# Ten gate tiles as five pairs of seven half-size products, and attention with one more pair in flight

## The chip, the core and the metric

The kernel runs on one core of a Trainium2 chip. The core has a matrix engine (TensorE, PE in the profile, its weight loads PEld), a vector engine (VectorE, DVE), an activation engine (ScalarE, ACT), a general engine (GpSimd, POOL) and a queue engine (SyncE, SP) that issues nearly all DMAs here. Engines run their own instruction streams in order and meet at semaphores. Matmuls write to the eight banks of PSUM; everything else lies in SBUF, in slabs of 128 partitions by 1032 float32.

The metric is the device time of one execution in microseconds, as a median of runs.

## The reference

One step of one layer of a decoder trunk, for a prompt of 1024 tokens and 8 sample tokens, in float32:

```
h = RMSNorm(x)
qa,ka,va,za, qb,kb,vb,zb, qc,zc, ga,gb,gc = split(h @ w_in)
y = x + W_out( sum_i sigmoid(g_i) * P_i( mixer_i(h) * silu(z_i) ) ),   i = A, B, C
```

Mixer A is dilated causal attention with 8 heads of 64 and three patterns of window and stride, mixer B sliding-window attention with 8 query heads on 2 key heads and a sink per head, mixer C attention into 256 memory tokens with 4 heads of 128. The sample tokens attend to caches of keys and values. The step also returns the new keys and values. What matters here: the gates g are three matrices of 1024 x 1024 columns of w_in, applied to all 1032 tokens (1024 of the prompt and 8 of the sample), and each only ever enters through its sigmoid, which the kernel makes from a tanh.

## The kernel before

Activations are kept transposed, features on partitions and tokens along the row. A matrix product in the kernel is a "tile": 128 output features for all 1032 tokens, in three chunks of CH = 344 tokens, with the contraction of 1024 in 8 blocks of 128. To hold float32 precision with the fast float32 format, each operand is split into a rounded high half and a remainder (`hh`, `hl` for activations, `wh`, `wl` for weights), and three of the four partial products are summed (`PARTS`, `order`, `fm`). A tile is therefore 3 chunks x 8 blocks x 3 = 72 matmuls of 344 columns, each with its own weight load. A branch tile has half the contraction.

The program is written out by a planner in Python. `Pace` is a model of the engines' clocks; `tick` is called between half chunks of a tile and issues side work when the model says that its inputs are there: a step of attention (`rope`), a step of the sample's attention (`samp`), weight fetches and splits (`wahead`, `wnext`, `wpump`), and callbacks left with `when`, which are tried at each tick. What is issued runs in that order on each engine; the model decides the order alone, while semaphores keep the data right.

The order of the dense work on TensorE is: memory keys and values; queries of C; then a list of jobs for B and A, with `fill` (12 z tiles, then 24 gate tiles) in between where a job isn't allowed yet; the remaining fill; then three branches (C, B, A: `branch`, 8 tiles each with 36 matmuls of 344 columns) and the output matrix (`out_phase`). `plan` inside `main` appends the weights of the next job when fewer than two weights are left in the list `W`, and appends the tail's weights (branches and output) once jobs and fill are used up. Weights are fetched `wdepth` ahead and split `wsoon` ahead.

A gate tile (`gate`) takes any of six PSUM banks in turn once attention is over (`dense`, `wide`), writes tanh of each chunk into a slab `sg`, and stores the slab to DRAM (`gsc`). The branches load it back later.

Attention runs in pairs of query blocks (`DuoC`, `DuoN`, `DuoR`; 112 in all). Each goes through a pipeline in `rope`: scores on TensorE into the one bank `psSc` (`s`), bias and softmax on DVE and ACT into `L` (`soft`), transposes into `psT` (`t_prev`, `t`), rounding and remainder of the probabilities (`hi`, `lo`), the product with values into `psO` (`pv`), and the eviction (`fin`). In `self.pipe = (new, p1)` two pairs are in flight: at each step the pair before the new one is transposed, and the one before that is multiplied with values. A step is skipped when the model says that `p1.L` or `p2.pl` isn't there yet. Up to three heads' inputs lie in slabs.

The sample's attention (`sample`, `samples`) is done on POOL (products `ck<-ck,qbc`, `cv<-cv,pb`) and DVE (reductions). After prompt attention has ended, two such samples run side by side, their row buffers in a slab (`late`), with all three key blocks fetched at once (`deep`).

The first branch needs mixer C's output times silu(z), split in halves (`y_fetch(2)`: loads `yr` and `zr` for four tiles, two at a time, product, split into `yh` and `yl`). It is called in `main` when fewer than four entries of fill are left.

`SLABS = 47` slabs are shared by all of this, and a slab is free again when the last Python name for it is dropped.

## Time and profile before

| | |
|---|---|
| median of 3 runs | 1166.72 us (1164.03 to 1168.59) |
| the profiled execution's own time | 1162.82 us |
| its span, first to last instruction | 1161.0 us |
| mean granted TensorE clock | 0.990 |
| DMA over the span | 206.29 MB, 178 GB/s |
| gate tiles: first and last store | 572.60 and 926.24 us |
| branches: stores of the gates loaded back | 926.7 to 1022.6 us |

Every helper of the kernel is recorded under one line (L150), so the profile is read by the names of tiles: `psD<-hh,wh` is a matmul that writes bank psD from activations hh and weights wh. Busy times of PE overlap from one matmul to the next, so the length of one matmul in a row (some 320 ns for 344 columns) is longer than the distance from one start to the next. `<-` behind a bracket names what ended an engine's idle time. SPq is the time that SP takes to issue a DMA, not the transfer.

### The profile page before, as it was taken

How to read it: one execution, taken by the hardware profiler on the slowest of the kernel's cores; microseconds unless marked ns; L12 is line 12 of the kernel's file. 1: busy time of each engine (PE TensorE's matmuls, PEld its weight loads, DVE VectorE, ACT ScalarE, POOL GpSimd, SP SyncE). 2: the span in 40 equal slices, each digit the busy share in tenths (PEclk: the TensorE clock that was granted, in tenths of full speed). 3: DMA queues.
4: the chain of work that ended last, by engine and by line, in shares of the span. 5: the costliest groups of instructions: out<-in, count | busy, mean ns of one | idle time of the engine just before them, and what ended most of it. 6: DMA issues, size and time to landing. Idle time of an engine off the chain costs nothing.

```text
span 1161.0 us, 19631 instructions
## 1 busy us (share of the span) xinstructions
PE 1125.8 (97%) x7424; PEld 1104.7 (95%) x7424; DVE 645.7 (56%) x1201; ACT 475.1 (41%) x1136; POOL 503.2 (43%) x402
## 2 busy tenths in 40 slices
PE   7899999999899999999999999999999999999998
PEld 7787999999899999999999999999999999999998
DVE  6754366444566867655755765643647447538211
ACT  6443355544555556556555455541212212213000
POOL 4454455232543232345235314423557665857200
PEclk8998999999999999999999999999999999999999
DMA  8312522399624555544654664648699699532332
GB/s 319 119 43 79 182 75 92 102 306 302 201 74 147 182 164 168 193 155 141 185 133 134 191 177 163 192 136 293 214 265 382 186 350 374 165 137 73 119 119 73
DMA packets 85794, 206.29 MB, mean 178 GB/s; under 512 B 13588, under 2 KB 38130, under 8 KB 85700
## 3 DMA queue, kind: packets, MB, share of 16 engines
q1 hardware_dynamic: 85556, 205.03, 54.6%
q8 instruction: 58, 0.95, 0.3%
q14 instruction: 36, 0.29, 0.1%
q10 hardware_dynamic: 144, 0.02, 0.0%
HBM read 154.98 MB, written 45.97 MB: 173 GB/s over the span
## 4 chain that ended last, share of the span: by engine, by line
PE 78%; DVE 6%; DMA 5%; POOL 4%; issue 3%; ACT 2%; SPq 1%; POOLq 0%; ACTq 0%; DVEq 0%
PE psD L150 46%; PE psO L150 14%; PE psSc L150 9%; PE psM L150 5%; PE psT L150 5%; DMA wr<-w_in 1%; DVE ml L150 1%; SPq L150 1%; DVE wl L150 1%; POOL sq L150 1%; DMA vhl<-vhl 1%; POOL c L150 1%; DMA bn<-rep 1%; DMA wr<-w_mk 1%; POOL wl L150 1%
## 5 line engine op out<-in xcount | busy, mean ns | idle before, releaser
L150 PE MATMUL psD<-hh,wh 128*128 128x344 f32 x1184 | 386.0, 326 | 3.9 <-DVE sz L150 1.7
L150 PE MATMUL psD<-hh,wl 128*128 128x344 f32 x1184 | 380.7, 322 | 4.7 <-DVE wl L150 4.7
L150 PE MATMUL psD<-hl,wh 128*128 128x344 f32 x1184 | 381.1, 322 | 2.3 <-POOL hl L150 1.4
L150 PEld LDWEIGHTS psD<-hh,wh 128*128 128x128 f32 x1184 | 224.1, 189 | 6.8 <-DVE sz L150 1.9
L150 PEld LDWEIGHTS psD<-hh,wl 128*128 128x128 f32 x1184 | 224.2, 189 | 5.3 <-DVE wl L150 5.3
L150 PEld LDWEIGHTS psD<-hl,wh 128*128 128x128 f32 x1184 | 224.4, 190 | 4.0 <-POOL hl L150 2.7
L150 POOL TENSOR_TENSOR wl<-wr,wh 128x1024 fp32r<-128x1024 f32 (+1 forms) x45 | 106.3, 2362 | 50.6 <-ACT wh L150 48.4
L150 ACT ACTIVATE p<-psT 128x512 fp32r<-128x512 f32 (+2 forms) x112 | 61.8, 552 | 93.5 <-PE psT L150 81.1
L150 DVE TENSOR_TENSOR wl<-wr,wh 128x1024 fp32r<-128x1024 f32 (+1 forms) x54 | 72.9, 1354 | 42.7 <-ACT wh L150 21.5
L150 ACT ACTIVATE wh<-wr 128x1024 fp32r<-128x1024 f32 (+1 forms) x62 | 54.7, 888 | 89.1 <-DMA wr<-w_out 36.9
L150 POOL TENSOR_TENSOR c<-raw 128x344 f32<-128x344 f32 x51 | 43.4, 851 | 96.1 <-ACT raw L150 85.8
L150 POOL TENSOR_TENSOR ck<-ck,qbc 128x1024 f32<-128x1024 f32 x24 | 65.3, 2733 | 39.6 <-DMA qbc<-d 21.6
L150 POOL TENSOR_TENSOR cv<-cv,pb 128x1024 f32<-128x1024 f32 x24 | 58.4, 2440 | 53.6 <-DMA pb<-d 28.8
L150 DVE TENSOR_TENSOR p<-psT,p 128x512 fp32r<-128x512 f32 (+2 forms) x112 | 70.7, 631 | 14.1 <-ACT p L150 13.4
L150 POOL TENSOR_SCALAR wh<-wr 128x1024 fp32r<-128x1024 f32 (+1 forms) x37 | 41.1, 1111 | 73.1 <-DMA wr<-w_in 43.6
L150 PE MATMUL psT<-ident,L 128*128 128x128 f32 x400 | 72.4, 272 | 0.0
L150 ACT ACTIVATE L<-L,sta 128x256 f32<-128x256 f32 (+1 forms) x128 | 59.5, 467 | 27.6 <-DVE sta L150 27.4
L150 POOL TENSOR_TENSOR sg<-sg,sg 128x344 f32<-128x344 f32 x48 | 55.1, 1155 | 34.4 <-DVE sg L150 19.4
L150 DVE CUSTOM_DVE_ANT_0 L<-psSc,bias 128x256 f32<-128x256 f32 (+1 forms) x128 | 43.7, 378 | 42.9 <-PE psSc L150 42.4
L150 ACT ACTIVATE sq<-psD 128x344 fp32r<-128x344 f32 x51 | 23.3, 457 | 74.7 <-PE psD L150 66.9
L150 POOL TENSOR_TENSOR sq<-c,sq 128x344 fp32r<-128x344 f32 x51 | 52.0, 1020 | 4.0
L150 PEld LDWEIGHTS psT<-ident,L 128*128 128x128 f32 x400 | 48.7, 140 | 0.2
(284 smaller groups left out, 2539.6 us busy)
## 6 DMA issues: line engine op xcount, KB each, us to landing
wr<-w_in SPq DMA_DIRECT2D x58, 512.0 KB
g<-sg SPq DMA_DIRECT2D x24, 516.0 KB
sg<-g SPq DMA_DIRECT2D x24, 516.0 KB
pb<-d SPq DMA_DIRECT2D x32, 256.0 KB
rb<-d SPq DMA_DIRECT2D x26, 258.0 KB
qbc<-d SPq DMA_DIRECT2D x12, 512.0 KB
z<-sz SPq DMA_DIRECT2D x12, 512.0 KB
wt<-d SPq DMA_DIRECT2D x24, 256.0 KB
```

Source lines behind the costliest of these rows:

```text
L150: r = f(*a, **k)
```

## The change

**Pairs of gate tiles.** The last gate tiles are computed two at a time. Two tiles are 256 output features; with the contraction of 1024 in two halves of 512 and the 1032 tokens in two halves of HT = 516, they are eight block products of 128 features x 512 x 516. The change computes them with seven products (Strassen's method in Winograd's form): sums and differences of blocks of the weights and of the activations are multiplied, and sums of the products give the four results. Each product is two token parts of 258 columns x 4 blocks x 3 partial products = 24 matmuls of 258 columns.

- `mix` (new) makes three sums of the activations' blocks (T1, T2, T4: 12 slabs `ht`) after attention has ended, while ordinary gate tiles still run, and sets a flag at its end; `mix_last` writes a fourth (T3) over the second token half of the first four activation slabs when the last ordinary gate is done.
- `pair_fetch` loads the two raw weight tiles, `pair_prep` makes the four sums on POOL and splits one operand after the other into a slab `wx`, `LEAD = 2` products ahead.
- `gate_pairs` runs the seven products, adds them up in PSUM and in slabs `u`, and writes tanh of the results; `gate_out` stores them.
- `plan` takes ordinary gates until the flag is set and their number is even; the rest go in pairs. Ten of the 24 tiles do.
- `y_fetch(2)` is called at the first product of the last pair; its splits wait for a flag `room`, set after that pair's fourth product, where the fetch of the tail's weights begins too.

**Attention.** `self.pipe` holds three pairs, so a pair is transposed two steps after its scores; `L`, `stc`, `stb` and `sta` get a third buffer, and slabs go from 47 to 46.

**Sample.** The side-by-side samples take a slab for their rows only if another one holds the row buffers (`rowbusy`), fetch one key block at a time (`deep = 1`), and a new one is begun only when the one before has been handed out (`feed`).

**z tiles.** tanh is written straight into the slab `sz`.

```diff
-        p1, p2 = self.pipe
+        p0, p1, p2 = self.pipe
...
-        if new and p1 and p1.carry:
-            new.prev = p1
+        if new and p0 and p0.carry:
+            new.prev = p0
...
-        self.pipe = (new, p1)
+        self.pipe = (new, p0, p1)
...
-        late = self.duos is None
-        deep = npat if late else 1
+        late = self.rowbusy
+        deep = 1
...
-            self.when([r], split, t, r)
+            self.when([r], self.after, "room", split, t, r)
...
+    def pair_prep(self, q):
...
+        if q == 0:
+            nc.gpsimd.tensor_add(z[:, :512], b[:, :512], b[:, 512:1024])
+            nc.gpsimd.tensor_sub(z[:, 512:1024], z[:, :512], a[:, :512])
+            src = a[:, :512]
...
+        elif q == 3:
+            y = st["y"] = self.slab(F32, "ws")
+            nc.gpsimd.tensor_sub(y[:, :512], a[:, :512], b[:, :512])
+            nc.gpsimd.tensor_sub(y[:, 512:1024], a[:, 512:1024], z[:, 512:1024])
+            src = a[:, 512:1024]
...
+        x = self.slab(F32R, "wx")
+        self.round(x[:, :512], src)
+        self.rest(x[:, 512:1024], src, x[:, :512])
+        self.pws.append((x[:, :512], x[:, 512:1024]))
+        self.pready += 1
+
+    def gate_pairs(self, pairs):
...
+        steps = (("B11", 0, True), ("T2", 1, True), ("T1", 2, True), ("B21", 0, False), ("T3", 1, False), ("T4", 1, False), ("B22", 2, False))
+        self.mix_last(h)
...
+        for p, pair in enumerate(pairs):
+            bank = [[self.ps("D", 2) for _ in range(2)], [self.ps("O", 2) for _ in range(2)], [self.ps("Sc", 1), self.ps("M", 1)]]
...
+            for q, (key, i, new) in enumerate(steps):
+                while self.pready < min(7 * p + q + LEAD, n):
+                    self.pair_prep(self.pready % 7)
+                if q == 2 and not last:
+                    self.pair_fetch(pairs[p + 1])
+                if q == 0 and last:
+                    self.y_fetch(2)
...
+                for j in range(2):
...
+                    for m, (y, z, k) in enumerate(self.order(4)):
+                        nc.tensor.matmul(b, w[y][:, k * P:(k + 1) * P], x[k][z][:, c], start=new and m == 0, stop=m == 11, skip_group_check=True)
+                    if q == 0:
+                        nc.scalar.activation(u1[:, c], b, AF.Copy)
+                    elif q == 1:
+                        nc.vector.tensor_tensor(u2[:, c], b, u1[:, c], op=ALU.add)
+                    elif q == 4:
+                        nc.vector.tensor_tensor(u3[:, c], b, u1[:, c], op=ALU.add)
+                        nc.vector.tensor_tensor(s2[:, d], bank[2][j][:, :HT // 2], u3[:, c], op=ALU.add)
+                    elif q == 3:
+                        nc.scalar.activation(s1[:, c], b, AF.Tanh, scale=0.5)
+                    elif q == 5:
+                        nc.vector.tensor_tensor(s2[:, c], b, u1[:, c], op=ALU.add)
+                    elif q == 6:
+                        nc.vector.tensor_tensor(s1[:, d], b, u2[:, c], op=ALU.add)
+                    yield
...
+                if q == 3 and last:
+                    self.flags.add("room")
+                    self.begin_tail()
...
-            while (jobs or fill) and len(self.W) - self.wi < 2:
+            while len(self.W) - self.wi < 2:
...
+                elif gates and ("mix" not in self.flags or len(gates) % 2):
+                    x, mt = gates.popleft()
+                    j = ([wi(34 + 8 * x + mt)], None, lambda x=x, mt=mt: self.gate(x, mt))
...
+            if self.duos is None and self.pipe == (None,) * 3 and "mixing" not in self.flags and len(gates) > 5:
+                self.flags.add("mixing")
+                self.mix()
...
+        if gates:
+            gates = list(gates)
+            yield from self.gate_pairs(list(zip(gates[::2], gates[1::2])))
```

## The prediction

> **What bounds the kernel.** I read the page's busy times first, then the busy times by stage, then what TensorE waited for.

> ```profile
> span 1161.0 us, 19631 instructions
> PE 1125.8 (97%) x7424; PEld 1104.7 (95%) x7424; DVE 645.7 (56%) x1201; ACT 475.1 (41%) x1136; POOL 503.2 (43%) x402
> ```

> ```profile
> 0.00:116.00 116.00, 100.17 (x541) 88.19 (x542) 70.08 (x95) 55.31 (x100) 55.43 (x54) 0.91 0.40 140
> 145.00:775.00 630.00, 619.01 (x4304) 613.15 (x4303) 383.13 (x860) 339.82 (x894) 242.65 (x202) 1.00 0.54 165
> 775.00:926.00 151.00, 150.42 (x961) 148.53 (x960) 78.69 (x84) 31.66 (x64) 82.47 (x52) 1.00 0.79 262
> 926.00:1063.00 137.00, 136.33 (x868) 136.07 (x867) 76.78 (x117) 29.77 (x46) 91.46 (x72) 1.00 0.67 237
> 1063.00:1161.00 98.00, 90.92 (x573) 89.78 (x571) 25.91 (x38) 9.87 (x17) 19.20 (x11) 1.00 0.27 92
> ```

> The columns are the length, busy PE, weight load, DVE, ACT and POOL with counts, the granted clock, the DMA share and GB/s. From 145 us on PE is full: attention among dense tiles (145 to 775) idles 11.0 us of 630, the gate tiles after it 0.6 of 151, the branches 0.7 of 137. The clock is at 1.00, so only fewer or shorter matmuls, or fewer waits, can shorten these stages. PE's own waits leave little there:

> ```profile
> PE psD L150 <- DVE wl L150: 5.6, 3, 2.4
> PE psD L150 <- DVE ml L150: 3.7, 3, 1.9
> ...
> PE psSc L150 <- DVE sta L150: 1.7, 2, 1.3
> PE psT L150 <- DVE aw L150: 1.7, 1, 1.7
> ```

> (total, times, longest). A bank that attention's softmax holds (sta) costs 1.7 us in all.

> **The change: the products.** Each gate tile is 72 matmuls of 344 columns. Its store follows its last product, and in a quiet stretch the stores stand one tile apart:

> ```profile
> 809.28 0.33 SPq L150 DMA_DIRECT2D g<-sg  x1
> ...
> 820.60 0.33 SPq L150 DMA_DIRECT2D g<-sg  x1
> ...
> 831.93 0.33 SPq L150 DMA_DIRECT2D g<-sg  x1
> ```

> That is 11.32 us a tile, 157.3 ns a matmul; ten tiles take 113.2 us. In place of them stand 5 pairs x 7 products x 24 = 840 matmuls of 258 columns (two token parts, four blocks of the contraction, three passes of the high and low halves): 168 a pair where there were 144, with a quarter fewer columns each. The trace has 256 columns in attention's scores, each with a weight load of its own:

> ```profile
> 182.61 0.28 PE L150 MATMUL psSc<-mkh,qh 128*128 128x256 f32 x1
> ...
> 183.20 0.28 PE L150 MATMUL psSc<-mkh,ql 128*128 128x256 f32 x1
> ...
> 755.24 0.88 PE L150 MATMUL psO<-p,v 128*128 128x128 f32 x6
> ```
> ```profile
> L150 PE MATMUL psO<-p,v 128*128 128x128 f32 x112 | 20.0, 260 | 0.0
> ```

> Six scores start within 0.59 us, 118 ns apart. The slope to 344 columns is (157.3-118)/88 = 0.45 ns a column, so 258 take 119 ns. Six 128-column products last 0.88 us; with the last one's own length (0.26 us, the mean of that group) taken off, five steps are 124 ns: below 256 columns nothing is won, and 124 is the high end here; the low end is a 256-column row without its two extra columns, 117. So the pairs take 840 x 119 = 100.0 us (98.3 to 104.2): **13.2 us less** (9.0 to 14.9).

> [...]

> **The weights of a pair.** Four sums of 512 columns on POOL and seven roundings and remainders of 512 replace two of 1024. A product's weights are prepared two ahead, and what is issued for product i+1 stands behind the evictions of i-1, so it has about one product, 24 x 119 = 2.86 us.

> ```profile
> L150 ACT ACTIVATE wh<-wr 128x512 fp32r<-128x512 f32 x24 | 14.8, 626 | 47.6 <-DMA wr<-w_brc 26.7 <-POOL sg L150 7.6 <-DVE yl L150 5.7
> L150 DVE TENSOR_TENSOR wl<-wr,wh 128x512 fp32r<-128x512 f32 x14 | 12.3, 880 | 0.0
> L150 POOL TENSOR_TENSOR wl<-wr,wh 128x512 fp32r<-128x512 f32 x12 | 20.7, 1721 | 10.4 <-ACT wh L150 9.7 <-DVE sg L150 0.7
> L150 DVE CUSTOM_DVE_ANT_0 L<-psSc,bias 128x256 f32<-128x256 f32 x88 | 35.2, 420 | 26.0 <-PE psSc L150 26.0
> ```

> Two evictions of 258 columns (2 x 0.42) beside the rounding (0.63), then the remainder on DVE (0.88): 1.7 us; on POOL 0.63 + 1.72 = 2.4. That fits, with 0.5 to 1.1 us to spare. The evictions add ten adds of 0.42 = 4.2 us of DVE a pair, in 20 us, and bank psO is written again one half product (1.43 us) after the product whose sum must first be read from it; two adds, 0.84, fit. What doesn't fit is a remainder that meets one of the sample's POOL products:

> ```profile
> 864.27 3.41 DVE L150 TENSOR_TENSOR wl<-wr,wh 128x1024 fp32r<-128x1024 f32 x1 [4.91 <-POOL wh L150]
> ...
> 870.43 1.21 DVE L150 TENSOR_TENSOR wl<-wr,wh 128x1024 fp32r<-128x1024 f32 x1
> ```

> The first ran while POOL worked on `cv<-cv,pb`, and took 2.2 us more. In this stage the ten such remainders on DVE average

> ```profile
> L150 DVE TENSOR_TENSOR wl<-wr,wh 128x1024 fp32r<-128x1024 f32 x10 | 16.1, 1613 | 28.2 <-POOL wh L150 15.2 <-ACT wh L150 13.1
> ```

> 0.4 us more than the undisturbed 1.21. In before a weight has a whole tile (11 us) of cover; now it has one product. Bounds: 0 (all hidden) to 35 x 0.4 = 14 us. Half of the 35 on DVE would lose 7 us without the spare time; it covers the most of it, so I take **3 us**.

> **From gates to branches.** Before, the first branch's inputs are fetched 58 us ahead of their use; now they are fetched at the start of the last pair, 7 x 2.86 = 20.0 us ahead, and split only after its fourth product.

> ```profile
> 867.81 0.37 SPq L150 DMA_DIRECT2D yr<-y  x1
> ```
> ```profile
> 874.09 1.22 DVE L150 TENSOR_TENSOR yr<-yr,zr 128x1024 f32<-128x1024 f32 x1 [0.63 <-DMA zr<-z]
> ...
> 903.91 1.43 DVE L150 TENSOR_TENSOR yl<-yr,yh 128x1032 fp32r<-128x1032 f32 x1 [1.92 <-ACT yh L150]
> ...
> 949.57 1.23 DVE L150 TENSOR_TENSOR yl<-yr,yh 128x1032 fp32r<-128x1032 f32 x1
> ```
> ```profile
> 876.69 2.39 POOL L150 TENSOR_TENSOR yr<-yr,zr 128x1024 f32<-128x1024 f32 x1 [3.95 <-DMA zr<-z]
> ```
> ```profile
> 879.51 1.06 ACT L150 ACTIVATE yh<-yr 128x1032 fp32r<-128x1032 f32 x1
> ```
> ```profile
> 875.00:900.00 25.00, 25.00 (x162) 24.67 (x161) 18.56 (x12) 7.30 (x12) 21.03 (x9) 1.00 0.97 379
> ```
> ```profile
> 925.56 0.32 PE L150 MATMUL psO<-yh,wh 128*128 128x344 f32 x1
> ```

> The chain took 867.81 to 905.34 = 37.5 us there, with nothing waiting for it. Its bare steps: the second tile lands and POOL begins its product after 8.9 us; that issues the fourth tile's load, another 8.9; product 2.39, rounding 1.06, remainder 1.23 (undisturbed, at 949.57): 23.5 us. PE then waits 23.5 - 20.0 = **3.5 us**; bounds 0 (loads that land faster than under the DMA share of 0.97 in that stretch) and 17.5 (the 37.5 again). The branch weights start at the same point, 3 products = 8.6 us ahead; their load, 0.63 and 0.88 lie inside that, and cost nothing beyond it unless SP's queue holds them up; then they are late beside the inputs, not after them.

> **Mixing the activations, and attention.** Four steps of one add on DVE, one on POOL, differences of 516 columns and three splits run beside two or three ordinary gate tiles, whose weights are two tiles ahead: 0 (bounds 0 and 2). With a third pair in flight, transposes use scores that are two steps old. PE saves at most the 1.7 us of `aw` and 1.7 of `sta` above, and new scores may wait for psSc's reader: 112 pairs at a tenth of 0.42 is 5 us. The pair before last's remainder must still be ready, and DVE issues it behind the reading of psSc, so I take 0 (bounds -3 and +5). Attention ends earlier, and that alone wins nothing: the same tiles are still to be done. It decides how many gates are left for pairs; each pair fewer costs 13.2 / 5 = 2.6 us. The third buffers cost one slab of 47, and the sample fetches one key block ahead instead of three; its last result has a long way to go:

> ```profile
> L150 DVE COPY ys<-sog x12: 171/171/172, 209.4 to 965.3; 128x8 f32<-128x8 f32 x12
> ```

> The last branch, which needs it, begins two branches of 8 x 36 matmuls x 157.3 ns = 45.3 us after 925.56, at 1016.2; 965.5 and a chain of 37.5 us give 1003.0, so some 13 us are to spare, and I take 0.

> **The sum.** -13.2 + 3 + 3.5 + 0 = -6.7 us on the profiled execution's 1162.82 (its span of 1161.0 and 1.8 around it): 1156.1. The median shown, 1166.72, lies 3.9 above that execution; the same difference gives **1160.0 us**.

> **Rivals.** (1) *All is hidden*: preparation and inputs keep up. For it: POOL is busy 82 of 151 us and DVE 79, and loads may land faster. Then -13.2 + 0 to 1: 1154. (2) *The inputs of the first branch are late*, the slower side: the chain of 37.5 us repeats, and PE stands 17.5 us at the head of the branches. For it: it is the one measured length; against: half of it was DVE held up by POOL with nobody waiting. -13.2 + 3 + 17.5 = +7.3: 1174. It decides from a wait of 13.2 - 3 = 10.2 us. (3) *The preparation bounds the products*: remainders held by POOL cost PE 0.4 us each, 14 in all: -13.2 + 14 + 3.5 = +4.3: 1171. Against: the spare time, and either engine may take a remainder. (4) *The spacing follows the number of matmuls*: at 139 ns, midway between 120 and 157, 840 take 116.8 us, +3.6 + 6.5: 1177; it turns at 113.2 / 840 = 135 ns. [...] (5) *The pairing hardly happens*, because attention ends late: with two pairs, -5.3 and +6: 1167. Against: attention's last scores are turned at 768.2, and the eleventh of the 24 gate stores follows at 774.98, so 13 tiles are still to go:

> ```profile
> L150 ACT ACTIVATE p<-psT x112: 366/598/603, 150.6 to 768.2; 128x512 fp32r<-128x512 f32 x72, 128x384 fp32r<-128x384 f32 x32, 128x256 fp32r<-128x256 f32 x8
> ```
> ```profile
> 774.98 0.33 SPq L150 DMA_DIRECT2D g<-sg  x1
> ```

> **Chances.** Forecast (1156 to 1164) 0.43, (1) 0.26, (2) 0.14, (3) 0.08, (4) 0.03, (5) 0.06. About 0.5% (5.8 us) is what a measurement of this kernel tells from no change. Faster: (1) and some six tenths of the forecast's case, 0.52. Slower (above 1172.5): most of (2), (4) and a third of (3), 0.18. Within: 0.30. The range is from (1) with attention's 3 us, 1151, to (2), 1174; the forecast's own is 1156 to 1164.

> **What would show it.** In the profile of the changed kernel: 840 matmuls of 258 columns, about 119 ns apart; five pairs of 20 us each plus waits named for `wx` (the preparation) summing to 3; a wait of about 3.5 us before the first product on `yh`, named for `yl` or `yh`; attention's waits on psSc unchanged near 2 us; from the first branch product to the end 1161.0 - 925.6 = 235 us as before. The prediction is wrong if the spacing is above 130 ns, if a wait over 10 us stands before the branches, if `wx` waits sum to over 8 us, or if the last branch waits for the sample.

## The result, and the profile after

The changed kernel takes 1180.7 us (median of 4, 1178.05 to 1181.02) against 1167.12 us for the kernel before on the same chip: 1.0123 times as long, 95% interval 1.0094 to 1.0152. The prediction was 1160.0 us in a range of 1151 to 1174; its sign was wrong, and so was its range. The profiled execution took 1180.44 us, 17.6 more than that of before; by the medians the change is 13.6 us, because the profiled execution of before lies 4.3 below its median. The terms below, which come from profiled executions, are known no better than that.

The head of the page of the changed kernel:

```profile
span 1178.6 us, 20121 instructions
PE 1126.5 (96%) x7544; PEld 1100.5 (93%) x7544; DVE 723.9 (61%) x1297; ACT 499.7 (42%) x1179; POOL 561.2 (48%) x439
```

PE is busy for 1126.5 us, where it was 1125.8. The saving in products doesn't show at all. Cut at the same points of the work (attention's bulk, the rest up to the last ten tiles, these ten, branches to the end), the busy times by stage of before are

```profile
722.00:812.40 90.40, 88.92 (x605) 87.93 (x604) 45.57 (x119) 35.34 (x102) 28.91 (x24) 1.00 0.63 201
812.40:925.60 113.20, 112.62 (x720) 110.89 (x719) 67.67 (x65) 25.54 (x49) 72.50 (x42) 1.00 0.79 264
925.60:1161.00 235.40, 227.65 (x1441) 226.26 (x1439) 102.69 (x154) 39.88 (x63) 110.66 (x82) 1.00 0.50 176
```

and of the changed kernel, whose pairs run from 810.2 to 936.9:

```profile
722.00:810.20 88.20, 82.40 (x504) 80.89 (x504) 62.24 (x60) 22.54 (x47) 52.52 (x34) 0.96 0.49 156
810.20:936.90 126.70, 111.91 (x864) 107.77 (x863) 90.11 (x120) 39.41 (x77) 101.59 (x66) 0.96 0.70 226
936.90:1178.60 241.70, 229.78 (x1442) 227.80 (x1440) 118.09 (x169) 42.12 (x66) 117.71 (x86) 0.99 0.54 186
```

The columns are those of the prediction: length, then PE, weight load, DVE, ACT and POOL, the granted clock, DMA share and GB/s. The start of the last ten tiles came 2.2 us earlier; these tiles took 13.5 us more (126.7 against 113.2) where 10.2 less was forecast; the rest took 6.3 more. Two columns tell what is new in the pairs: PE busy leaves 14.8 us of the 126.7 idle (126.7 - 111.9), and the clock is at 0.96. POOL's work in this stage went from 72.5 to 101.6 us.

PE's own waits (total, times, longest):

```profile
PE psD L152 <- DVE wl L152: 8.2, 6, 2.2
PE psD L152 <- DVE wx L152: 4.6, 3, 2.0
PE psO L152 <- ACT wx L152: 3.8, 2, 2.6
...
PE psO L152 <- DVE u L152: 3.6, 4, 2.8
PE psD L152 <- DVE yl L152: 3.5, 2, 2.4
...
PE psO L152 <- POOL wx L152: 2.1, 2, 1.3
PE psSc L152 <- ACT L L152: 2.1, 2, 1.5
```

Waits for `wx`, the weights of a product, sum to 10.8 us, on three engines; the prediction had 3, and named over 8 as a sign of being wrong. In the last ten tiles of before PE waited for a weight once, for 0.6 us: there a weight had a whole tile, 11.3 us, of cover.

**The spacing is as forecast.** PE's timeline, an undisturbed product and then one that follows waits:

```profile
813.10 3.04 PE L152 MATMUL psO<-ht,wx 128*128 128x258 f32 x24
815.98 1.75 PE L152 MATMUL psSc<-ht,wx 128*128 128x258 f32 x12
...
821.38 0.51 PE L152 MATMUL psD<-hh,wx 128*128 128x258 f32 x2 [1.99 <-DVE wx L152]
...
825.53 0.38 PE L152 MATMUL psO<-hh,wx 128*128 128x258 f32 x1 [1.24 <-ACT wx L152]
...
827.32 0.74 PE L152 MATMUL psO<-hh,wx 128*128 128x258 f32 x2 [1.29 <-POOL wx L152]
...
866.35 0.50 PE L152 MATMUL psO<-ht,wx 128*128 128x258 f32 x2 [2.60 <-ACT wx L152]
867.69 4.42 PE L152 MATMUL psO<-ht,wx 128*128 128x258 f32 x22 [0.85 <-POOL wx L152]
871.95 1.61 PE L152 MATMUL psSc<-ht,wx 128*128 128x258 f32 x12
```

24 matmuls of 258 columns run from 813.10 to the next start at 815.98: 120 ns each (119 forecast), so 840 make 100.8 us. The 22 after the wait at 867.69 take 4.26 us up to 871.95, 194 ns each: behind the wait the matmuls themselves are slow. The granted clock in short windows (columns: length, busy PE, clock, DMA share, GB/s) says the same for such places (the first and the last of three):

```profile
827.00:831.00 4.00, 3.68 (x18) 0.57 0.00 0
...
885.00:889.00 4.00, 3.95 (x20) 0.57 0.32 122
```

So the 126.7 us are 100.8 of matmuls, 14.8 of waits (10.8 for `wx`, 3.6 for `u`, the rest small), about 4.5 that the three slow stretches add (each 3.4 us at some 215 ns instead of 120), and 6.6 that I did not take apart. In these lie the last matmul's own length ahead of each wait, and 24 small matmuls of the sample.

**Why the weights are late.** POOL's timeline, then ACT's, then DVE's, around the waits from 821 to 828:

```profile
815.60 7.99 POOL L152 TENSOR_TENSOR ck<-ck,qbc 128x1024 f32<-128x1024 f32 x3
823.55 1.27 POOL L152 TENSOR_TENSOR ws<-wr,wr 128x512 f32<-128x512 f32 x1
824.78 1.26 POOL L152 TENSOR_TENSOR ws<-wr,ws 128x512 f32<-128x512 f32 x1
826.01 1.26 POOL L152 TENSOR_TENSOR wx<-ws,wx 128x512 fp32r<-128x512 f32 x1
```
```profile
824.85 0.63 ACT L152 ACTIVATE wx<-ws 128x512 fp32r<-128x512 f32 x1 [8.54 <-DVE lg L152]
```
```profile
815.53 0.68 DVE L152 TENSOR_TENSOR wx<-ws,wx 128x512 fp32r<-128x512 f32 x1
...
827.34 2.81 DVE L152 TENSOR_TENSOR wx<-wr,wx 128x512 fp32r<-128x512 f32 x1 [2.50 <-POOL wx L152]
```

Three products of the sample hold POOL for 7.99 us. The sums of a pair's weights stand behind them, ACT's rounding behind the sums, and PE behind both. (ACT's row names `lg`, DVE's reduction of the sample, which ended at 824.84; the first sum ended at 824.82. Which of the two held the rounding the row doesn't tell; both stand behind the sample's products.) The whole lead is two products, 5.8 us. The wait of 1.99 us at 821.38 came by another road: DVE's remainder, begun at 819.96, stood in DVE's order behind a reduction for which DVE had been idle for 1.95 us, until POOL's product was there. The wait at 860.85 (1.63 us) came the same way, behind 2.41 us. The last row is the case that the prediction had priced: DVE's remainder, from 827.34, took 2.81 us beside a product of the sample on POOL (`ck<-ck,qbc`, 2.37 us from 827.23), where its like took 0.68.

### The profile page after: what moved, and what is told of

Its sections match the earlier page's. It is cut to its first block, busy times and chain, and to the rows that moved or that the text cites. A ratio compares the mean times of both kernels' runs of the same rounds, so it can differ in the third digit from the quotient of the medians.

```text
span 1178.6 us, 20121 instructions
## 1 busy us (share of the span) xinstructions
PE 1126.5 (96%) x7544; PEld 1100.5 (93%) x7544; DVE 723.9 (61%) x1297; ACT 499.7 (42%) x1179; POOL 561.2 (48%) x439
## 5 line engine op out<-in xcount | busy, mean ns | idle before, releaser
L152 PE MATMUL psD<-hh,wh 128*128 128x344 f32 x1040 | 340.5, 327 | 2.0 <-ACT hh L152 1.3
L152 PE MATMUL psD<-hh,wl 128*128 128x344 f32 x1040 | 334.8, 322 | 5.0 <-DVE wl L152 5.0
L152 PE MATMUL psD<-hl,wh 128*128 128x344 f32 x1040 | 335.0, 322 | 2.4 <-POOL hl L152 1.4
L152 PEld LDWEIGHTS psD<-hh,wl 128*128 128x128 f32 x1040 | 197.2, 190 | 5.8 <-DVE wl L152 5.8
L152 PEld LDWEIGHTS psD<-hh,wh 128*128 128x128 f32 x1040 | 197.6, 190 | 4.9 <-ACT hh L152 1.8
L152 PEld LDWEIGHTS psD<-hl,wh 128*128 128x128 f32 x1040 | 197.6, 190 | 4.0 <-POOL hl L152 2.7
L152 POOL TENSOR_TENSOR wl<-wr,wh 128x1024 fp32r<-128x1024 f32 (+1 forms) x37 | 84.4, 2283 | 48.3 <-ACT wh L152 42.4
L152 ACT ACTIVATE wh<-wr 128x1024 fp32r<-128x1024 f32 (+1 forms) x57 | 50.0, 881 | 92.2 <-DMA wr<-w_out 38.1
L152 POOL TENSOR_TENSOR ck<-ck,qbc 128x1024 f32<-128x1024 f32 x24 | 61.0, 2548 | 46.1 <-DMA qbc<-d 36.1
L152 POOL TENSOR_TENSOR cv<-cv,pb 128x1024 f32<-128x1024 f32 x24 | 61.3, 2555 | 42.3 <-DMA pb<-d 14.8
L152 POOL TENSOR_TENSOR sg<-sg,sg 128x344 f32<-128x344 f32 x48 | 54.5, 1146 | 26.3 <-DVE sg L152 21.4
L152 POOL TENSOR_SCALAR wh<-wr 128x1024 fp32r<-128x1024 f32 (+1 forms) x32 | 36.6, 1143 | 52.6 <-DMA wr<-w_in 29.1
L152 POOL TENSOR_TENSOR sq<-c,sq 128x344 fp32r<-128x344 f32 x51 | 52.6, 1032 | 4.0
```

What stands on the lines that cost most here:

```text
L152: r = f(*a, **k)
```

## The experiments

Each list of a time and a ratio is the median and the ratio to the kernel before on the same chip, with its 95% interval. Edits are to the changed kernel unless said otherwise. First I took the change apart.

**1. No pairs.** All gates as ordinary tiles; the tail is fetched as before, the third pair in flight stays.

```
-  ... and "mixing" not in self.flags and len(gates) > 5:
+  ... and "mixing" not in self.flags and len(gates) > 99:
+  if not fill and len(gates) < 4 and not self.ys_:
+      self.flags.add("room"); self.y_fetch(2)
```

> All 24 gates as ordinary tiles, the first branch's inputs fetched before the last gates as in the kernel before; attention with three pairs in flight, the sample's changes and 46 slabs stay. Theory A (the whole loss lies in the pairs and at the passage from them to the branches): 1163 to 1169 us, the time of the kernel before. Theory C (the attention or sample part costs too): 1172 us or more.

1154.31 us, 0.9894 (0.9869 to 0.9920). Its stages, cut at the same points:

```profile
722.00:804.50 82.50, 82.50 (x532) 81.72 (x531) 34.16 (x49) 14.01 (x34) 41.48 (x28) 1.00 0.63 211
804.50:917.70 113.20, 113.20 (x725) 112.08 (x724) 45.84 (x54) 22.35 (x45) 55.31 (x36) 1.00 0.74 244
917.70:1153.60 235.90, 228.04 (x1442) 226.51 (x1440) 103.72 (x155) 40.11 (x63) 108.23 (x84) 1.00 0.52 181
```

Both theories missed: the time is below that of before. So the pairs as a whole cost 25 us (1178.6 - 1153.6): 5.7 ahead of them (810.2 against 804.5), 13.5 in them, 5.8 behind them. The rest of the change gains 7.4 us of span, which the prediction had put at nothing; by the medians (1167.41 for before on this chip) it gains 13.1. This is the fastest kernel here that computes everything.

**2. Two pairs of attention in flight**, products in pairs kept (`p1, p2 = self.pipe`, as before).

> Two pairs in flight in attention as before, the rest of the change kept; attention ends later, so fewer gates may be left for pairs. Theory A: each pair costs about 2.3 us more than two tiles did, so 1176 to 1181 us, nearer to 1176 if there are fewer pairs. Theory C: 1170 us or less.

1194.84 us, 1.0266 (1.0218 to 1.0315), above both theories. With attention ending later only three pairs of tiles are left, and still it is 14 us slower than with five. The last branch waits 11 us for its inputs: the sample, whose last result (`ys`) comes at 1042.7, is late.

**8. Before, with only the third pair in flight** (`p0, p1, p2`, the third buffers, 46 slabs):

> The kernel before with only the third pair in flight in attention, its third buffers, 46 slabs and the z tile's tanh in place: no pairs, the sample as before. Theory B (the third pair in flight takes PE's waits out of the attention stage): 1154 to 1160 us, as in the run without pairs. Rival (it was the sample's new order): 1164 us or more.

1157.83 us, 0.9917 (0.9896 to 0.9938). With experiment 1 this shows the gain twice; the third pair, its buffers and the z tile's tanh are in both, and which of them gains what was not run. PE's waits from 145 to 775 us in before, without `sta` and `aw` (1.7 each), which the prediction showed:

```profile
PE psD L150 <- DVE wl L150: 2.4, 1, 2.4
...
PE psD L150 <- DVE sz L150: 1.7, 1, 1.7
PE psM L150 <- POOL sq L150: 1.6, 3, 0.7
PE psT L150 <- DVE lg L150: 1.1, 1, 1.1
PE psD L150 <- ACT wh L150: 1.0, 1, 1.0
```

Attention ends at 722 us in experiment 1, at 768 in before. In experiment 1 4.1 us of these 11.2 are left up to there, and from there to 775 us PE waits for nothing; the largest is new, 2.1 us for psSc's reader (`ACT L`). The prediction had counted `sta` and `aw` alone. Those for weights, z and the mean of squares went too.

**3. Without the sample of mixer A** (its results are zeros), pairs kept:

```
-  yield (lambda t=t: self.sample(0, t, ...))
+  self.nc.vector.memset(self.ys[:, t], 0.0); self.flags.add(("ys", 0, t)); yield ()
```

> Leaves out mixer A's attention of the 8 sample tokens (its outputs are set to zero), and nothing else. Theory A1 (the preparation of the weights is late because it stands behind the sample's products on POOL and is locked out by them): the five pairs take 106 us or less instead of 124.8, and the whole 1158 to 1165 us. Theory A2 (the preparation is late by itself, its own chain being longer than a product): the pairs stay at 118 us or more, the whole above 1172.

1151.53 us, 0.9892 (0.9817 to 0.9968); the pairs take 104.9 us (805.11 to 909.97), and no wait for `wx` is left. So it is the sample's work beside the pairs that makes the weights late; which part of it (POOL, DVE, loads) this run alone doesn't tell.

**4. Weights four products ahead** (`LEAD = 4`):

> Weights of a pair prepared four products ahead instead of two (LEAD 4), nothing else. Theory A1 with the short cover as its point: waits named for wx fall from 10.8 us to 4 or less and the whole to 1168 to 1174 us. Rival (the queues of DVE and POOL are simply full in this stretch, so an earlier issue stands in the same queue): wx waits only move to other names, 1177 us or more.

1193.52 us, 1.0251 (1.0187 to 1.0315): slower again. The pairs do shrink, to 114.5 us, and the waits for `wx` are gone; but the waits for `u` (the bank of the fifth product, read by DVE before the sixth may write it) are 6.1 us, and the last branch stands still. PE's waits from 800 to 1100 us:

```profile
PE psD L152 <- ACT yh L152: 15.5, 1, 15.5
PE psO L152 <- DVE u L152: 6.1, 4, 3.0
```

**9. The sample's products on DVE** from the mixing on (`nc.vector` for `nc.gpsimd` in the two `tensor_mul` of `sample`), two products ahead:

> The changed kernel, with the sample's products of keys and values on DVE (1.2 us each, no lock against DVE's own adds) instead of POOL (2.4 us) once the mixing has begun. Theory A1 in its sharper form (it is POOL's long sample products, first in POOL's queue and then as a lock on DVE's two-input adds, that make the weights late): the pairs take 105 to 115 us instead of 124.8, the whole 1160 to 1172 us. Rival (the pairs' side work fills DVE as it is, so 29 us of sample products more on DVE cost as much): the pairs 122 us or more, the whole 1178 or more.

1173.07 us, 1.0061 (1.0032 to 1.0090); 118.6 us up to the first branch product, of which 114.2 to the pairs' last one: between the two forecasts, nearer to the theory. POOL's queue was part of it; 4.6 us of waits for `wx` on POOL stay.

**10 and 11. The order of the products changed** so that bank psO is written again one product later (third, fourth, fifth product: T1, T3, B21 instead of T1, B21, T3; the preparation of the fourth and fifth weights is exchanged too), with `LEAD = 4`; 11 adds the edit of 9.

> LEAD 4, and the fourth and fifth product of a pair change places, so that a whole product stands between the one whose sums DVE must read from bank psO and the next one that writes this bank. If the four waits for u of 2.5 to 3.0 us in the run with LEAD 4 come from that short distance, they fall below 2 us in all and the pairs take 104 to 108 us; the whole still carries the late sample at the last branch (15 us there), so 1172 to 1188. Rival (the adds are late by more than a product): u waits stay above 5 us.

> Both: LEAD 4 with the products' places changed, and the sample's products on DVE. Theory A1: pairs 102 to 106 us, no wait for the sample at the last branch, the whole 1146 to 1156 us, below the kernel without pairs (1154). Rival: DVE's load makes the sample or the adds late, above 1165 us.

10: 1201.28 us, 1.0302 (1.0263 to 1.0342). 11: 1190.62 us, 1.0220 (1.0182 to 1.0259). In 10 the waits for `u` are gone and the pairs take 105.9 us up to their last product, as expected, but the last branch waits 32.3 us. In 11 the pairs are what the prediction wanted:

```profile
809.70:911.80 102.10, 102.10 (x854) 101.52 (x853) 74.22 (x104) 31.11 (x59) 70.00 (x54) 1.00 0.67 213
```

102.1 us, without a wait and at full clock: 24.6 us less than in the changed kernel. Yet the kernel became slower by 10, because of the last branch (PE's timeline):

```profile
1026.51 0.66 PE L152 MATMUL psD<-yh,wh 128*128 128x344 f32 x1 [14.51 <-ACT yh L152]
...
1041.67 0.66 PE L152 MATMUL psD<-yh,wh 128*128 128x344 f32 x1 [12.96 <-ACT yh L152]
```

It waits for the sample of mixer A, whose `ys` comes last (a row of the tile's instructions, first and last start: the changed kernel, then 11):

```profile
L152 DVE COPY ys<-sog x12: 171/172/2257, 224.6 to 1000.5; 128x8 f32<-128x8 f32 x12
```
```profile
L152 DVE COPY ys<-sog x12: 171/171/538, 223.9 to 1037.7; 128x8 f32<-128x8 f32 x12
```

**12 and 14. Two attempts at that wait, on top of 11**: the first branch's inputs fetched half a pair earlier (12), and all three key blocks of the sample fetched at once (14, `deep = npat if self.duos is None else 1`).

> As the run before, with the first branch's inputs fetched from the fourth product of the last pair but one on, 23 products ahead of the branches less 12, 1.4 times as early... that is 11 products or 31 us ahead instead of 20. If the inputs' chain is what PE waits for at the passage (4.8 us in the changed kernel), 2 to 4 us less than the run before; if the waits there are for the branch weights, no change.

> LEAD 4, changed places and DVE products again, with the sample as in the run that was late (no early start), but all three key blocks fetched at once after attention, as in the kernel before. If the fetch of one block at a time made the sample late, the waits at the last branch (27 us) fall below 8 and the whole to 1160 to 1170 us; if not, within 4 us of 1190 or above.

12: 1200.03 us, 1.0307 (1.0273 to 1.0341); 35 us of waits at the last branch, and 9 us longer than 11, which neither forecast allowed. 14: 1180.11 us, 1.0136 (1.0093 to 1.0179); 7.3 us there, where 11 had 27.5. `ys` comes at 1029.2, 8.5 us earlier, so the fetch of one block at a time is part of the delay. But the last branch also begins 13 us later: behind the pairs, ahead of the first branch, PE waits 9.0 us for the sample's scores (`lg`), whose transposes stand there in its order.

**5, 6, 13, 15 and 7. The sample started early**, beside attention (`many = True`, and mixer B's samples handed out like A's): alone (5), with `LEAD = 4` (6), on 11 (13), on 11 with the first branch's inputs and the tail fetched earlier (15), and without pairs (7).

> The changed kernel, but the sample tokens' B and A attention may run two at a time from the start, so that mixer A's part is over, or nearly, when the pairs begin; all work is done. Theory A1 (POOL's sample products hold up the pairs' preparation): the pairs take 104 to 110 us instead of 124.8 and the whole 1150 to 1160 us. Rival A3 (DVE, POOL and DMA are as full without them, and what leaves the pairs is paid for in attention): above 1168 us.

> As the run before, with the weights of a pair prepared four products ahead. Theory A1: with the sample gone the cover of two products is already enough, so within 3 us of the run before; if what is left of the waits is for wx, up to 4 us less.

> The pairs with LEAD 4, the products' places changed, the sample's products on DVE from the mixing on, and the sample two at a time from the start. Theory S (with the weights on time, the pairs' gain of some 11 us is lost only through the sample, which becomes late for the last branch): pairs 102 to 104 us, no wait over 2 us at the last branch, the whole 1148 to 1156 us. Rival R (the pairs take the slabs, queues and DVE time that the sample needs, so that it comes late however early it begins): a wait of over 8 us at the last branch, the whole above 1164 us.

> The run with early sample, LEAD 4, changed places and DVE products, with the first branch's inputs fetched 11 products ahead of the branches instead of 7, and the branch weights and the splits begun one product earlier. If what the pairs win is now lost at the passage to the branches (waits of 12 us there in that run), these fall to 6 us or less and the whole to 1158 to 1166 us. If the side work of this stretch only moves on, the waits appear behind the passage or at the last branch and the whole stays above 1168 us.

> Early sample, all 24 gates as ordinary tiles. Theory A1: the pairs without the sample beside them gain 3 to 8 us on ordinary tiles, so this one is 3 to 8 us slower than the run with early sample and pairs; about 1154 to 1160 us. Rival (pairs never pay): this one is faster.

5: 1178.98 us, 1.0107 (1.0088 to 1.0126). 6: 1180.04, 1.0118 (1.0092 to 1.0145). 13: 1173.41, 1.0069 (1.0044 to 1.0094). 15: 1175.26, 1.0083 (1.0057 to 1.0110). 7: 1163.95, 0.9975 (0.9952 to 0.9998). In 5 mixer A's sample still ran inside the pairs (`ys` last at 950.1), which took 125.2 us: the edit did not move what it was meant to move, and 5 and 6 say little of the theory. In 13 the wait at the last branch is gone, and the pairs take 108.2 us; four waits of 0.5 to 3.4 us stand at the passage to the branches instead, so neither of its two accounts holds whole. In 15 one wait of 3.3 us is left at the passage and one of 3.6 stands at the last branch: the waits moved on. 7 is 15 us faster than 5, where 3 to 8 us slower was forecast; its rival, that the pairs don't pay, came out. The early start itself costs: 7 is 9.6 us slower than 1.

**16 and 17. The best case of the pairs**: the order of 10 without mixer A's sample (16), and no pairs without that sample (17).

> Leaves out mixer A's attention of the sample tokens (its outputs are zero); pairs with LEAD 4 and the products' places changed. Theory S: with the sample gone the pairs keep their gain, 4 to 9 us below the run without pairs that leaves out the same part. Rival R2 (mixing and passage eat the gain even so): within 3 us of it, or above.

> Leaves out mixer A's attention of the sample tokens (its outputs are zero); all 24 gates as ordinary tiles. PE's own share of that sample is small and the kernel without pairs waited for it nowhere, so 1150 to 1156 us by both theories; it is the base for the run before.

16: 1153.95 us, 0.9908 (0.9883 to 0.9932). 17: 1149.74 us, 0.9875 (0.9851 to 0.9899). Stages of 16, then of 17:

```profile
722.00:808.30 86.30, 81.85 (x500) 80.49 (x500) 66.94 (x67) 22.72 (x46) 56.06 (x33) 0.96 0.42 132
808.30:909.10 100.80, 100.80 (x843) 100.80 (x842) 41.03 (x68) 24.20 (x44) 69.41 (x64) 1.00 0.40 142
909.10:1150.20 241.10, 231.90 (x1441) 229.89 (x1440) 107.60 (x147) 41.67 (x66) 105.53 (x81) 0.98 0.47 167
```
```profile
722.00:801.40 79.40, 79.40 (x511) 79.09 (x510) 25.56 (x42) 11.58 (x28) 25.30 (x17) 1.00 0.46 149
801.40:914.60 113.20, 113.20 (x721) 113.20 (x720) 21.51 (x15) 18.55 (x35) 22.75 (x21) 1.00 0.37 129
914.60:1149.50 234.90, 227.63 (x1442) 226.49 (x1440) 97.16 (x140) 39.40 (x62) 102.65 (x78) 1.00 0.48 170
```

Here the products gain nearly all of what was forecast, 12.4 us of 13.2. Some 6.9 are lost ahead of them while the activations are mixed, and 6.2 behind them at the passage: nothing is left, as the rival had it (by the medians 16 is 4.2 us slower, and the two intervals overlap). The mixing on PE's timeline of the changed kernel, where it runs too:

```profile
751.39 0.28 PE L152 MATMUL psT<-ident,aw 128*32 128x128 f32 x1 [2.29 <-DVE aw L152]
...
752.84 0.49 PE L152 MATMUL psO<-hl,wh 128*128 128x344 f32 x1
753.13 0.49 PE L152 MATMUL psO<-hh,wl 128*128 128x344 f32 x1
...
761.41 0.43 PE L152 MATMUL psD<-hh,wl 128*128 128x344 f32 x1 [2.21 <-DVE wl L152]
```

DVE has 62 us of work in the 88 before the pairs (34 in experiment 1), and the ordinary tiles' remainders come late behind the sums. At 753 the matmuls of 344 columns stand 0.29 us apart instead of 0.157.

## Why the prediction was wrong

It was a sum of five terms; by stages of the profiled executions they came to:

| term | forecast, us | measured, us |
|---|---|---|
| the products (840 x 119 ns) | -13.2 | -12.4 by spacing (120 ns; 100.8 in 16) |
| the weights of a pair (measured: all of the pairs' stage beyond the products) | +3 (0 to 14) | +25.9 |
| from gates to branches | +3.5 (0 to 17.5) | +6.3 |
| mixing the activations | 0 (0 to 2) | +5.7 |
| attention with a third pair (measured: start of the last ten tiles in experiment 1 against before) | 0 (-3 to +5) | -7.9 |
| sum | -6.7 | +17.6 |

- **The products: right.** 258 columns take 120 ns. The rival by which the spacing follows the number of matmuls is refuted: at 139 ns the 840 would take 116.8 us, and experiment 16 shows 100.8.
- **The weights of a pair: the step that failed.** The prediction compared one product's time (2.86 us) with the undisturbed durations of its preparation (1.7 to 2.4) and called the rest spare; for the disturbed case it priced only a remainder that meets POOL, at a mean of 0.4 us. What the runs show is a queue: the sums stand behind up to three of the sample's products on POOL (7.99 us), against a lead of 5.8. Experiment 3 takes the sample away and the pairs lose 21.8 us; 11 reaches 102.1 us with the sample kept. Its rival (3), preparation bounds the products, was the right mechanism. Its bound of 14 us held for the waits on `wx` (10.8, and some 3 in two slow stretches behind them) but not for the stage (25.9). The 0.84 us of adds that were to fit ahead of the sixth product didn't always fit: 3.6 us of waits for `u`, 2.8 of them in one place. The row behind the bound was a mean over ten remainders that nobody was waiting for.
- **A wait costs more than its length.** The prediction summed waits. In six places behind waits, from 752.3 to 946.9 us, the granted clock was 0.50 for 3.41 us, and each cost some 1.5 us more, an estimate from the spacings in them (215 ns instead of 120, and 287 instead of 157 for 344 columns). That was in none of the terms.
- **From gates to branches: the direction right, the size too small.** In the changed kernel the listed waits there are 1.36, 2.44 and 1.02 us (4.8) and one slow stretch makes up the rest. They name a branch weight's remainder as well as the inputs; the prediction had taken the weights to be late beside the inputs, not on top of them. Its sum was also off by itself: the bare steps that it lists add to 22.5 us and not 23.5, which makes its wait 2.5 us.
- **Mixing: wrong.** The cover named, weights two tiles ahead, did not hold. The sums raise DVE's share of that stage to 62 of 88 us, and the sample's and the tiles' small steps come late behind them.
- **Attention: wrong, to the other side.** Only the two waits named for attention were counted; the bound of -3 left out every other wait of the stage. Without the pairs the change is a gain of 0.8 to 1.1% (experiments 8 and 1).
- **The sample in the last branch: right for this kernel, by luck.** PE didn't wait there. But the prediction left `ys` at the 965.5 of before and put the branch at 1016.2; it came at 1000.5, and the branch began at 1034.5 because everything ahead was late. As soon as the pairs are faster (4, 10, 11) the last branch comes 15 to 24 us earlier, `ys` 34 to 49 later, and the branch waits 15 to 32 us for it. The second pair of mixer A's samples starts to load keys at 838.53 in experiment 1, 875.75 in the changed kernel and 908.09 in experiment 11. The fetch of one key block at a time is 8.5 us of it (14 against 11). What else delays it stays open: slabs, the planner's view of POOL and DVE, and SP's order could each do it, and none of the runs separates them.

So the trade was this. PE's time went down by 12.4 us of products; DVE and POOL, which had been free to run late, took on the sums, and the three places where they are now needed at once (mixing, weights, passage) cost 38 us. Mending one place moved the time to the next: the pairs' waits became the last branch's. Even with mixer A's sample out of the way the pairs gain nothing over ordinary tiles (16 against 17, 1153.95 and 1149.74 us). Whether another schedule of the sums could change that was not tried beyond these runs.

## What to carry to other kernels

A trade of matmuls for additions is to be priced on the engine that adds, as a queue: take the longest run of other work that can stand ahead of the new step, from a row of the timeline, and compare it with the lead, not the undisturbed durations with the mean spare time. When an engine works ahead of PE, a step is cheap because of its lead; a change that shortens the lead changes the price of every row that was measured before it. And where a part of a change can be run by itself, run it: here the half that the prediction had put at zero was the gain. Last, look for what comes behind a wait that is mended: here it was the sample, and no run of the pairs that computes everything beat ordinary tiles.

## What the hardware showed that was not expected

**One long DVE step held the next matmul.** DVE's timeline of the changed kernel:

```profile
881.93 0.16 DVE L152 TENSOR_TENSOR sog<-spsf,vsa 128x8 f32<-128x8 f32 x1
882.13 2.34 DVE L152 TENSOR_TENSOR sog<-sog 128x8 f32<-128x8 f32 x1
...
884.58 0.42 DVE L152 TENSOR_TENSOR u<-psO,u 128x258 f32<-128x258 f32 x1
```

An addition of 8 columns took 2.34 us (0.17 at 881.85), as long as POOL's product `cv<-cv,pb` beside it (882.10 to 884.44). Behind it in DVE's order stood the reading of psO, and behind that PE, which waited 2.80 us.
